# Gate, up and down projections as seven products of half size in place of eight, in a hybrid decoder layer on one core

## The chip, the core and the metric

The kernel runs on one core of a Trainium2 chip. The core has TensorE (PE; PEld is its weight load), VectorE (DVE), ScalarE (ACT), GpSimd (POOL), SyncE (SP, which only issues transfers here) and 16 DMA engines. [...] The metric is device time in microseconds (us); the median of a few runs counts.

## The reference

One decoder layer in float32: 512 tokens, width 2048, inner width 5632. The first half (two mixing branches and their output projection) is not changed. The second half is

```
h = modulate(rms_norm(x, norm_ffn_g[l]), sh_f, sc_f)
gate, up = jnp.split(h @ w_gu[l], 2, axis=-1)
x = x + g_f[:, None, :] * ((jax.nn.silu(gate) * up) @ w_down[l])
...
return rms_norm(x, final_norm_g)
```

`modulate` is h * (1 + scale) + shift. Shift, scale and the gate g_f are columns of silu(c) @ w_ada + b_ada, one value for each feature.

## The kernel before

Features lie on partitions, the 512 tokens (S) on the free axis; the width is 16 tiles of 128 (KT), the inner width 44 (FT). Each float32 operand is split into two float32r parts, hi and lo, and a product is three matmuls, hi by hi, hi by lo, lo by hi (`mm3`, L124 to L126). SP loads a weight block (`wraw`, L115), ACT casts it to `whi` (L105), DVE subtracts it to `wlo` (L106).

`channel` does the second half. It first puts half of the output projection on x1 (`project`, weights `w_out`; DVE adds the gated result to x1, `square` sums squares). Beside it, `mod_steps` works out columns 68 to 79 of the modulation: a load `adaq` and a DVE product with accumulation (L199) for each quarter column. Then `norm` gives 1/rms in PSUM, and `modulate` makes hi and lo of h (L247, L251, L252). Four chunks of the inner width follow: for eleven tiles each, gate and up (16 k-tiles, weights stationary, 512 tokens moving), Silu on ACT, product and split; then 16 output tiles of the down projection over the chunk's eleven k-tiles, added to x1 with the gate (L969). PSUM accumulators take turns over three tags. After the last chunk come `norm` again, the final scaling (L975) and a write of each x1 tile (L977).

Pools: `big` is 32 tiles of 128 x 512 (x1, the mixing half's operands, later h). The weights have pool `wm` (512 columns, three buffers), and from the norm on pool `wf` (1024 columns; two raw buffers, three of hi and of lo). Instructions stand on each engine in the order that a scheduler gives them, from program order, priorities (the splits of weights have high priority) and buffers that come free; each engine then works its queue in order.

## Time and profile before

| | us |
|---|---|
| median of 3 runs | 2512.97 |
| lowest, highest run | 2510.55, 2514.32 |
| span of the profiled execution | 2515.8 |
| start of the gate/up part (first matmul) | 1046.0 |
| last large matmul | 2494.2 |

The span is what one profiled execution took from its first to its last instruction; it lies 2.8 us above the median. A row of a group reads: line, engine, operation, output<-inputs with shapes and count, then busy time and mean ns of one, then idle time before it and what ended it. A row of the timeline reads: start, duration, engine, line, operation, and in brackets the idle time before and its releaser. The page gives a granted TensorE clock of 0.986 of full speed over the span; most of what is missing lies in the mixing half and at the end.

### The profile page before, as it was taken

What the parts mean: (1) busy time and instruction counts of PE and PEld (TensorE: products, weight loads), DVE (VectorE), ACT (ScalarE), POOL (GpSimd) and SP (SyncE); (2) the same over time, 40 slices, a digit from 0 to 9 for tenths busy, and PEclk for the clock granted to TensorE, in tenths of its full rate; (3) what the DMA queues carried; (4) which work ended last, traced back from release to release, by engine and by line L of the source; (5) the groups of instructions that cost most, each with busy time, mean ns of one, the idle gap of its engine ahead of it and who ended that gap; (6) DMA issues with size and microseconds to landing.
All of it is one profiled execution on the core that took longest, in us unless ns stands there. A gap on an engine that the chain in (4) does not pass through costs nothing.

```text
span 2515.8 us, 30983 instructions
## 1 busy us (share of the span) xinstructions
PE 2413.9 (96%) x11560; PEld 1953.4 (78%) x11560; DVE 1380.4 (55%) x3111; ACT 843.7 (34%) x1340; POOL 82.0 (3%) x131
## 2 busy tenths in 40 slices
PE   5999999999999999899999999999999999999997
PEld 3677777877777886687788888888888888888885
DVE  7979898999969847854423322233322233222244
ACT  4357364455355333432222222222222222222221
POOL 0000111111101000000000000000000000000000
PEclk9999998999999999999999999999999999999998
DMA  8864444444342438366423332323333233333233
GB/s 304 308 219 130 148 128 143 131 152 144 125 135 81 143 108 283 119 195 194 160 90 95 108 100 93 101 83 98 106 98 99 89 92 105 101 93 100 85 95 112
DMA packets 138938, 333.22 MB, mean 132 GB/s; under 512 B 15458, under 2 KB 28898, under 8 KB 134690
## 3 DMA queue, kind: packets, MB, share of 16 engines
q1 hardware_dynamic: 138788, 331.25, 40.7%
q8 instruction: 90, 1.47, 0.2%
q14 instruction: 60, 0.49, 0.1%
HBM read 322.92 MB, written 7.87 MB: 131 GB/s over the span
## 4 chain that ended last, share of the span: by engine, by line
PE 72%; DVE 9%; DMA 7%; issue 1%; ACT 1%; SPq 0%; POOL 0%; DVEq 0%; ACTq 0%
PE ps_mm L124 10%; PE ps_mm L126 10%; PE ps_mm L125 10%; PE ps_gr L126 6%; PE ps_st L124 6%; PE ps_gr L124 6%; PE ps_st L126 6%; PE ps_gr L125 6%; PE ps_st L125 6%; DMA adaq<-in_w_ada 6%; DVE adaq L199 2%; DVE wlo L106 2%; DVE rw_xp L764 1%; DVE rw_x L766 1%; DMA wraw<-in_w_out 1%
## 5 line engine op out<-in xcount | busy, mean ns | idle before, releaser
L106 DVE TENSOR_TENSOR wlo<-wraw,whi 128x1024 fp32r<-128x1024 f32 (+2 forms) x552 | 496.7, 902 | 730.2 <-ACT whi L105 721.1
L105 ACT CAST whi<-wraw 128x1024 fp32r<-128x1024 f32 (+2 forms) x552 | 436.6, 792 | 1292.4 <-PE ps_mm L125 401.1
L124 PE MATMUL ps_mm<-hhi,whi 128*128 128x512 f32 x1020 | 417.1, 410 | 9.8 <-ACT hhi L251 7.2
L126 PE MATMUL ps_mm<-hhi,wlo 128*128 128x512 f32 x1020 | 407.2, 399 | 1.7 <-DVE wlo L106 1.6
L125 PE MATMUL ps_mm<-hlo,whi 128*128 128x512 f32 x1020 | 406.5, 399 | 0.8 <-DVE hlo L252 0.7
L124 PEld LDWEIGHTS ps_mm<-hhi,whi 128*128 128x128 f32 x1020 | 193.4, 190 | 53.2 <-ACT hhi L251 9.9
L125 PEld LDWEIGHTS ps_mm<-hlo,whi 128*128 128x128 f32 x1020 | 193.7, 190 | 43.4 <-DVE hlo L252 4.8
L126 PEld LDWEIGHTS ps_mm<-hhi,wlo 128*128 128x128 f32 x1020 | 193.8, 190 | 42.3 <-DVE wlo L106 3.0
L199 DVE SCALAR_TENSOR_TENSOR adaq<-adaq,cbq 128x512 f32<-128x512 f32 x256 | 173.5, 687 | 92.9 <-DMA adaq<-in_w_ada 85.1
L126 PE MATMUL ps_gr<-hhi,wlo 128*128 128x512 f32 x496 | 193.7, 390 | 3.1 <-DVE wlo L106 3.1
L126 PE MATMUL ps_st<-hhi,wlo 128*128 128x512 f32 x496 | 193.6, 390 | 2.0 <-DVE wlo L106 2.0
L124 PE MATMUL ps_st<-hhi,whi 128*128 128x512 f32 x496 | 194.0, 391 | 1.6 <-ACT hhi L251 1.6
L125 PE MATMUL ps_gr<-hlo,whi 128*128 128x512 f32 x496 | 193.5, 390 | 0.0
L125 PE MATMUL ps_st<-hlo,whi 128*128 128x512 f32 x496 | 193.5, 390 | 0.0
L124 PE MATMUL ps_gr<-hhi,whi 128*128 128x512 f32 x496 | 192.6, 391 | 0.0
L126 PEld LDWEIGHTS ps_gr<-hhi,wlo 128*128 128x128 f32 x496 | 93.4, 188 | 23.6 <-DVE wlo L106 4.1
L126 PEld LDWEIGHTS ps_st<-hhi,wlo 128*128 128x128 f32 x496 | 93.4, 188 | 21.8 <-DVE wlo L106 2.5
L124 PEld LDWEIGHTS ps_st<-hhi,whi 128*128 128x128 f32 x496 | 93.5, 188 | 21.6 <-ACT hhi L251 2.2
L125 PEld LDWEIGHTS ps_gr<-hlo,whi 128*128 128x128 f32 x496 | 93.7, 189 | 19.6
L124 PEld LDWEIGHTS ps_gr<-hhi,whi 128*128 128x128 f32 x496 | 93.7, 189 | 19.4
L125 PEld LDWEIGHTS ps_st<-hlo,whi 128*128 128x128 f32 x496 | 93.3, 188 | 19.8 <-DVE hlo L252 0.3
L766 DVE TENSOR_TENSOR rw_x<-rw_x,rw_xp 128x27 f32<-128x27 f32 (+23 forms) x496 | 94.7, 196 | 5.7
(312 smaller groups left out, 3809.6 us busy)
## 6 DMA issues: line engine op xcount, KB each, us to landing
wraw<-in_w_gu SPq DMA_DIRECT2D x176, 512.0 KB, 3.6
adaq<-in_w_ada SPq DMA_DIRECT2D x256, 256.0 KB, 3.3
wraw<-in_w_in SPq DMA_DIRECT2D x160, 256.0 KB, 3.0
ada<-in_w_ada SPq DMA_DIRECT2D x32, 1024.0 KB, 7.2
wraw<-in_w_down SPq DMA_DIRECT2D x64, 512.0 KB, 3.5
wraw<-in_w_out SPq DMA_DIRECT2D x64, 256.0 KB, 3.3
wraw<-in_w_down SPq DMA_DIRECT2D x64, 192.0 KB, 2.3
x<-in_x SPq DMA_DIRECT2D x32, 256.0 KB, 5.3
```

The lines of the kernel that those rows point to most:

```text
L105: nc.scalar.copy(out=hi, in_=src)
L106: nc.vector.tensor_tensor(out=lo, in0=src, in1=hi.bitcast(F32), op=ALU.subtract)
L124: mm(ps, lhsT=w[0], rhs=x[0], start=start, stop=False)
L125: mm(ps, lhsT=w[0], rhs=x[1], start=False, stop=False)
L126: self.pe = mm(ps, lhsT=w[1], rhs=x[0], start=False, stop=stop).ins
L199: nc.vector.scalar_tensor_tensor(out=t, in0=t, scalar=1.0, in1=cb, op0=ALU.mult, op1=ALU.mult, accum_out=part[:, m, h:h + 1])
L764: tt(out=pr[:, :n, :j], in0=at[:, s + 1:, s:s + 1].to_broadcast([P, n, j]), in1=x[:, s:s + 1, :j].to_broadcast([P, n, j]), op=ALU.mult)
L766: tt(out=x[:, s + 1:, :j], in0=x[:, s + 1:, :j], in1=pr[:, :n, :j], op=ALU.add)
```

## The change

Gate/up and down are now done by a Strassen-Winograd form. A and B are cut into two by two blocks: A by tokens (256 each) and by k, B by k and by columns. Seven products of half size replace eight; their operands are sums of blocks, and the results are sums of products.

The operands change places: 128 k x 128 tokens of an activation operand are stationary, 128 k x 512 columns of weights move, so results come with tokens on partitions. A "block" m is 512 columns of gate and the same 512 of up (eleven blocks, eight k-tiles for each half of K), or for down two blocks of 2 x 512 output columns in each of three chunks of K (8, 7 and 7 k-tiles per half). `half` does a block in two passes of steps of two k-tiles: products 1, 6, 5, 4, then 7, 2, 3. Each step loads weights (512 KB a load, four in the first pass, three in the second), adds them on DVE (`wraw<-wraw,wraw`, L1269, L1270, L1276 and L1285), splits each product's operand and issues twelve matmuls (L1227 to L1229), six for each of two token tiles. `finish` takes products out of PSUM: p1 by ACT (L1237), the others by DVE (p6 L1240, p5 L1243, p4 L1246, p7 L1249 and L1250, p2 L1254, p3 L1257). Products 1 and 7 share two PSUM banks, 6 and 2 two, 5 and 3 two, 4 has two.

The activation operands are built once: for h in the first block, with subtractions on POOL (`h_first`, `h_second`), for the silu products (which go to DRAM and come back, `from_s`) during the last block of the stage before. As results now lie by tokens, the silu products and x1 are transposed on PE (`flip`: four transposes, an ACT copy, a write to DRAM): sixteen groups for x1 beside the output projection, four for each gate/up block in the next block's first step. Down results of the three chunks are added through DRAM (`yd`, POOL, L1091); with the last chunk come the gate as a row of DRAM (`gf`, L1096), x1 read back (L1097), and the squares (ACT); after all, the scalings (L1172) and writes. Columns 80 to 95 of the modulation are worked out during gate/up. The pool `wm` is closed before the second half of the output projection, and `wf` has eight raw buffers and four of hi and lo. The weights are packed in the new blocks, and the output is by tokens. The rest of the diff takes comments out and puts `big` into eight tiles of four.

```diff
@@ channel @@
+        self.wmctx.close()
+        self.open_weights(ctx, "wf", 1024, 8, 4)
...
-        self.open_weights(ctx, "wf", 1024, 2, 3)
...
+        def flip(dst, tag, srcs):
+            ps = self.ps(tag)
+            for z, v in enumerate(srcs):
+                nc.tensor.transpose(ps[:, z * P:(z + 1) * P], in_=v, identity=self.con("ident"))
+            t = fq.tile([P, S], F32, tag="ft", name="flip", bufs=2)
+            nc.scalar.copy(out=t, in_=ps)
+            nc.sync.dma_start(out=dst, in_=t)
+        def flip_x1(e):
+            for t in range(4):
+                flip(self.x1d[t][e], "ch", [xt[4 * e + z][:, t * P:(t + 1) * P] for z in range(4)])
...
+            def done(m):
+                self.square(acc, xt[m], m, fp)
+                if m % 4 == 3 and m < KT - 1:
+                    flip_x1(m // 4)
...
-                pg, pu = ps(), ps()
-                self.gemm(pg, i["w_gu"][2 * m], h)
-                self.gemm(pu, i["w_gu"][2 * m + 1], h)
-                t = fp.tile([P, S], F32, tag="ft", name="sil", bufs=2)
-                act(out=t, in_=pg, func=AF.Silu)
-                p = ps()
-                self.gemm(p, i["w_down"][cf, m], s)
-                stt(out=xt[m], in0=p, scalar=self.mod[:, 80 + m:81 + m], in1=xt[m],
-                    op0=ALU.mult, op1=ALU.add)
...
+            rstd = self.norm(acc, "ch")
+            flip_x1(3)
...
+        def h_first(j):
+            q, z = j // 2, slice(2 * (j % 2), 2 * (j % 2) + 2)
+            for a in (q, 2 + q):
+                for k in range(z.start, z.stop):
+                    v, kk = quads[a][:, k], 4 * a + k
+                    stt(out=v, in0=v, scalar=self.cols[:, 16 + kk:17 + kk], in1=rstd, op0=ALU.mult, op1=ALU.mult)
+                    nc.scalar.activation(out=v, in_=v, func=AF.Identity, bias=self.mod[:, 48 + kk:49 + kk])
+            a11, a21 = quads[q][:, z, :256], quads[q][:, z, 256:]
+            a22 = quads[2 + q][:, z, 256:]
+            t = self.staging()
+            s1, s2 = t[:, :2], t[:, 2:]
+            pool_tt(out=s1, in0=a21, in1=a22, op=ALU.subtract)
+            pool_tt(out=s2, in0=s1, in1=a11, op=ALU.subtract)
+            ops = stages[0]["ops"]
+            for p, v in ((1, a11), (4, a22), (5, s1), (6, s2)):
+                if j % 2 == 0:
+                    ops[p, q] = self.operand_tile(p)
+                self.split_into(ops[p, q][:, 0, z], ops[p, q][:, 1, z], v)
...
+        def from_s(st, c, q, second):
...
+                a11 = load(0, 0)
+                operand(1, a11)
+                a21, a22 = load(0, 1), load(1, 1)
+                operand(4, a22)
+                pool_tt(out=a21, in0=a21, in1=a22, op=ALU.subtract)
+                pool_tt(out=a11, in0=a21, in1=a11, op=ALU.subtract)
+                operand(5, a21)
...
+        def gu_end(m, a, v, w, u, t):
+            act = nc.scalar.activation
+            if u is not None:
+                act(out=w, in_=w, func=AF.Silu)
+                tt(out=w, in0=w, in1=u, op=ALU.mult)
+                self.sT[t + 2] = w
...
+                    rows = list(self.sT)
+                    def pending(z):
+                        flip(where[4 * m + z], ("st", "y")[z % 2], [r[:, z * P:(z + 1) * P] for r in rows])
...
+        def fetch(src, tag):
+            t = fq.tile([P, S], F32, tag=tag[0], name="fetch", bufs=tag[1])
+            nc.sync.dma_start(out=t, in_=src)
+            return t
+        def down_end(c):
+            def put(x, t, e):
+                if c:
+                    pool_tt(out=x, in0=x, in1=fetch(yd[t][e], ("ft", 2)), op=ALU.add)
+                if c < 2:
+                    nc.sync.dma_start(out=yd[t][e], in_=x)
+                    return
+                g = fetch(self.gf[:, e * S:(e + 1) * S].to_broadcast([P, S]), ("ad", 2))
+                tt(out=x, in0=x, in1=g, op=ALU.mult)
+                tt(out=x, in0=x, in1=fetch(self.x1d[t][e], ("ft", 2)), op=ALU.add)
+                junk = fq.tile([P, S], F32, tag="ad", name="junk", bufs=2)
+                nc.scalar.activation(out=junk, in_=x, func=AF.Square, accum_out=ss[:, t, e:e + 1])
+                if e % 2 == 0:
+                    nc.sync.dma_start(out=self.xd[t][e // 2], in_=x)
+                else:
+                    kept[t, e] = x
...
+        stages = [dict(n=8, count=11, src=gu_src, end=gu_end, ops={})]
+        for c in range(3):
+            stages.append(dict(n=chunks[c][1], count=2, src=down_src(c), end=down_end(c), ops={}))
...
+        for z, st in enumerate(stages):
+            for m in range(st["count"]):
+                final = m == st["count"] - 1
+                for second in (False, True):
+                    if not z and not m and second:
+                        h_second()
+                    steps = self.half(st, m, second)
+                    for j in range(4):
+                        if not z and not m and not second:
+                            h_first(j)
+                        next(steps)
+                        if final and z + 1 < len(stages) and j % 2:
+                            from_s(stages[z + 1], z, j // 2, second)
+                        if z == 0 and m:
+                            next(mods, 0)
...
+        r = self.small.tile([P, 4], F32, tag="rstd", name="rstd", bufs=1)
+        nc.vector.tensor_reduce(out=r, in_=ss, op=ALU.add, axis=AX.X)
+        nc.scalar.activation(out=r, in_=r, func=AF.Sqrt, scale=1.0 / D, bias=self.eps[:, 0:1])
+        nc.vector.reciprocal(out=r, in_=r)
+        for t in (2, 3, 0, 1):
+            for e in range(4):
+                x = kept[t, e]
+                stt(out=x, in0=x, scalar=r[:, t:t + 1], in1=fg[:, e], op0=ALU.mult, op1=ALU.mult)
+                nc.sync.dma_start(out=self.out[t, :, e * S:(e + 1) * S], in_=x)
@@ new functions of Layer @@
+    def half(self, stage, m, second):
...
+        tags = {1: ("mm", "mm"), 6: ("gr", "gr"), 5: ("ch", "ch"), 4: ("st", "y"),
+                7: ("mm", "mm"), 2: ("gr", "gr"), 3: ("ch", "ch")}
...
+        def product(p, b, k0, w):
+            with tc.high_priority():
+                hi = self.wp.tile([P, self.wc], F32R, tag="whi", name="whi", bufs=self.wb[1])
+                lo = self.wp.tile([P, self.wc], F32R, tag="wlo", name="wlo", bufs=self.wb[1])
+                hi, lo = (t.rearrange("p (k n) -> p k n", n=S)[:, :w] for t in (hi, lo))
+                self.split_into(hi, lo, b)
+            o = stage["ops"][p, k0 // 4]
+            if k0 == 0:
+                ps[p] = [self.ps(tags[p][t]) for t in range(2)]
+            for t in range(2):
+                for z in range(w):
+                    k = k0 + z
+                    ah, al = (o[:, h, k % 4, t * P:(t + 1) * P] for h in range(2))
+                    mm(ps[p][t], lhsT=ah, rhs=hi[:, z], start=k == 0, stop=False)
+                    mm(ps[p][t], lhsT=al, rhs=hi[:, z], start=False, stop=False)
+                    mm(ps[p][t], lhsT=ah, rhs=lo[:, z], start=False, stop=k == n - 1)
+                if k0 + w == n:
+                    finish(p, t)
+        def finish(p, t):
+            keep, q = self.keep, ps[p][t]
+            if p == 1:
+                x = keep["a", t] = tmp("a", t)
+                nc.scalar.copy(out=x, in_=q)
+            elif p == 6:
+                x = keep["b", t] = tmp("b", t)
+                tt(out=x, in0=q, in1=keep["a", t], op=ALU.add)
+            elif p == 5:
+                x = keep["v", t] = tmp("v", t)
+                tt(out=x, in0=q, in1=keep["b", t], op=ALU.subtract)
+            elif p == 4:
+                x = keep["w", t] = tmp("w", t)
+                tt(out=x, in0=q, in1=keep["b", t], op=ALU.add)
+            elif p == 7:
+                u, v, w = tmp("b", t), keep["v", t], keep["w", t]
+                tt(out=w, in0=q, in1=w, op=ALU.add)
+                tt(out=u, in0=v, in1=q, op=ALU.subtract)
+                stage["end"](m, None, None, w, u, t)
+            elif p == 2:
+                x = keep["a", t]
+                tt(out=x, in0=q, in1=x, op=ALU.add)
+            else:
+                x = keep["v", t]
+                tt(out=x, in0=q, in1=x, op=ALU.add)
+                stage["end"](m, keep["a", t], x, None, None, t)
+        for k0 in range(0, n, 2):
+            w = min(2, n - k0)
+            flips = None
+            if not second and k0 == 0:
+                flips, self.pending = self.pending, None
+            if not second:
+                b11, b12, b22, b21 = (load(z, k0, w) for z in (0, 2, 3, 1))
+                product(1, b11, k0, w)
+                with tc.high_priority():
+                    tt(out=b11, in0=b11, in1=b12, op=ALU.add)
+                    tt(out=b12, in0=b11, in1=b22, op=ALU.add)
+                product(6, b12, k0, w)
+                if flips:
+                    flips(0)
+                    flips(1)
+                with tc.high_priority():
+                    tt(out=b21, in0=b21, in1=b12, op=ALU.add)
+                product(5, b11, k0, w)
+                if flips:
+                    flips(2)
+                    flips(3)
+                product(4, b21, k0, w)
+            else:
+                b12, b22, b21 = (load(z, k0, w) for z in (2, 3, 1))
+                with tc.high_priority():
+                    tt(out=b12, in0=b12, in1=b22, op=ALU.add)
+                product(7, b12, k0, w)
+                product(2, b21, k0, w)
+                product(3, b22, k0, w)
+            yield```

On DVE, at the change from one gate/up block to the next (`wraw_11133`, `_11135`, `_11137`, `_11139` are the new block's first weights; `ps_mm_10900` and `_10901` are product 7 of the block before, `wlo_11112` is the lo part of its product 3), the changed kernel has:

```order
L106 TENSOR_TENSOR wlo_11112<-wraw_11062,whi_11111 128x1024
L106 TENSOR_TENSOR wlo_11142<-wraw_11133,whi_11141 128x1024
L1249 TENSOR_TENSOR ev_w_10851<-ps_mm_10900,ev_w_10851 128x512
L1269 TENSOR_TENSOR wraw_11133<-wraw_11133,wraw_11135 128x1024
L1250 TENSOR_TENSOR ev_b_11077<-ev_v_10831,ps_mm_10900 128x512
L1270 TENSOR_TENSOR wraw_11135<-wraw_11133,wraw_11137 128x1024
L1064 TENSOR_TENSOR ev_w_10851<-ev_w_10851,ev_b_11077 128x512
L1276 TENSOR_TENSOR wraw_11139<-wraw_11139,wraw_11135 128x1024
L106 TENSOR_TENSOR wlo_11162<-wraw_11135,whi_11161 128x1024
L106 TENSOR_TENSOR wlo_11197<-wraw_11133,whi_11196 128x1024
L106 TENSOR_TENSOR wlo_11231<-wraw_11139,whi_11230 128x1024
L1249 TENSOR_TENSOR ev_w_10859<-ps_mm_10901,ev_w_10859 128x512
```

The second tile of product 7 leaves PSUM (last row) behind four splits and three additions of the new block's weights. On PE, at the same place, the new block's first products stand directly behind product 3:

```order
L1229 MATMUL ps_ch_10937<-wlo_11112,comb_10886 128x512
L1227 MATMUL ps_mm_11145<-whi_11141,comb_10464 128x512
...
L1229 MATMUL ps_mm_11145<-wlo_11142,comb_10464 128x512
L1227 MATMUL ps_mm_11146<-whi_11141,comb_10464 128x512
L1228 MATMUL ps_mm_11146<-whi_11141,comb_10464 128x512
```

`ps_mm_11146` takes the bank of `ps_mm_10901`. Before, DVE had at the end of a gate/up pair one product (L958) between splits, and the next accumulator was another bank:

```order
L106 TENSOR_TENSOR wlo_11831<-wraw_11828,whi_11830 128x1024
L958 TENSOR_TENSOR sil_11789<-sil_11789,ps_gr_11668 128x512
L106 TENSOR_TENSOR wlo_11861<-wraw_11858,whi_11860 128x1024
L106 TENSOR_TENSOR slo_11793<-sil_11789,shi_11792 128x512
L106 TENSOR_TENSOR wlo_11891<-wraw_11888,whi_11890 128x1024
```

On SP, at the end of the output projection and the start of gate/up, before:

```order
L115 DMA wraw_9752<-in_w_out 128x512
L115 DMA wraw_10508<-in_w_gu 128x1024
...
L115 DMA wraw_10252<-in_w_out 128x512
L115 DMA wraw_10538<-in_w_gu 128x1024
L115 DMA wraw_10270<-in_w_out 128x512
L115 DMA wraw_10568<-in_w_gu 128x1024
```

and in the changed kernel (`x1d03` to `x1d33` are the writes of the last flips of x1):

```order
L943 DMA x1d03_9430<-flip_10381 128x512
L198 DMA adaq_12579<-in_w_ada 128x512
L943 DMA x1d13_9434<-flip_10389 128x512
L1211 DMA wraw_10476<-in_w_gu 128x2x512
L943 DMA x1d23_9438<-flip_10397 128x512
L943 DMA x1d33_9442<-flip_10405 128x512
L1211 DMA wraw_10478<-in_w_gu 128x2x512
L1211 DMA wraw_10480<-in_w_gu 128x2x512
L1211 DMA wraw_10482<-in_w_gu 128x2x512
```

The first gate/up weights stood among the loads of `w_out`; now they stand behind the last writes of x1.

More of the change, by code (lines that the diff above doesn't have):

```diff
@@ L973, in channel @@
-        rstd = self.norm(acc, "ch")
-        for k in range(KT):
-            stt(out=xt[k], in0=xt[k], scalar=self.vec("final_norm_g", k), in1=rstd,
-                op0=ALU.mult, op1=ALU.mult)
-            nc.sync.dma_start(out=self.out[:, k], in_=xt[k])
+        def flip(dst, tag, srcs):
[5 more added lines that the diff above has]
+            nc.sync.dma_start(out=dst, in_=t)
```

223 lines of the change are left out of this document (161 added, 62 removed).

## The prediction

> **What bounds the kernel now.** First the page's head and its chain of work that ended last; then the windows, engine by engine.
>
> ```profile
> span 2515.8 us, 30983 instructions
> PE 2413.9 (96%) x11560; PEld 1953.4 (78%) x11560; DVE 1380.4 (55%) x3111; ACT 843.7 (34%) x1340; POOL 82.0 (3%) x131
> ...
> PE 72%; DVE 9%; DMA 7%; issue 1%; ACT 1%; SPq 0%; POOL 0%; DVEq 0%; ACTq 0%
> ```
>
> TensorE (PE) is busy nearly always. A share over the whole span hides stages, so two windows (span start and width, then busy time and count of PE, PEld, DVE, ACT, POOL, then clock, DMA share, GB/s):
>
> ```profile
> 400.00:600.00 200.00, 192.15 (x1129) 152.29 (x1129) 183.11 (x610) 103.66 (x199) 21.45 (x31) 0.97 0.47 147
> 1400.00:1600.00 200.00, 200.00 (x884) 165.61 (x883) 58.96 (x58) 48.09 (x55) 0.00 (x0) 1.00 0.31 99
> ```
>
> In the gate/up/down part PE has no gap: 200 us over 884 matmuls is 0.2262 us each, VectorE (DVE) is busy 29%, POOL not at all. Fewer matmuls are worth their full time there, as long as another engine does not become the bound. The other window shows how dense DVE gets in this kernel: 92%, never 100%.
>
> **The change, part by part.** *Matmuls.* Gate, up and down issue (1408 + 704) x 3 = 6336 matmuls of 512 columns; seven products for eight leave 5544, of the same 512 columns. 792 x 0.2262 = **179 us** less. All else is cost.
>
> *DVE.* Its rows:
>
> ```profile
> L106 DVE TENSOR_TENSOR wlo<-wraw,whi 128x1024 fp32r<-128x1024 f32 x239 | 292.6, 1225 | 451.8 <-ACT whi L105 445.8
> L105 ACT CAST whi<-wraw 128x1024 fp32r<-128x1024 f32 x239 | 251.7, 1054 | 786.2 <-PE ps_gr L125 196.7 <-PE ps_st L125 196.1 <-PE ps_mm L125 191.8
> L958 DVE TENSOR_TENSOR sil<-sil,ps_st 128x512 f32<-128x512 f32 x15 | 10.3, 687 | 42.7 <-PE ps_st L126 42.7
> ```
> ```profile
> 1059.18 2.36 DVE L106 TENSOR_TENSOR wlo<-wraw,whi 128x1024 fp32r<-128x1024 f32 x2 [1.83 <-ACT whi L105]
> ...
> 2501.37 10.62 DVE L975 SCALAR_TENSOR_TENSOR x<-x,vecs,ps_ch 128x512 f32<-128x512 f32 x16 [1.58 <-PE ps_ch L240]
> ```
>
> Two subtractions in a row end 2.36 - 1.225 = 1.135 us apart, sixteen operations of 512 take 10.62, 0.664 each: these are the rates in a full queue. A column block m of gate/up (eight k-tiles) has four steps, each with seven splits and four additions of weights, 44 x 1.135 = 49.9 us, and 18 operations of 512 (evictions L1237 to L1257, silu products), 11.9: **DVE needs 61.8**. PE needs 28 products x 12 matmuls = 336 x 0.2262 = **76.0**. Blocks m1 to m9 stay with PE (six adaq operations beside them do not change that). For a down block of seven k-tiles it is 294 x 0.2262 = 66.5 against 54.
>
> *Transposes.* Sixteen groups of four for x1, 44 for the silu products:
>
> ```profile
> 219.35 0.48 PE L124 MATMUL ps_mm<-lru_uhi,whi 128*128 128x512 f32 x1
> 219.67 0.62 PE L655 MATMUL ps_st<-cons,bd_b 128*128 128x128 f32 x4
> 220.05 0.48 PE L125 MATMUL ps_mm<-lru_ulo,whi 128*128 128x512 f32 x1
> ```
>
> Four 128x128 products between two large ones spread these from 0.226 to 0.70 us: 0.47 a group, 1.9 a block.
>
> *The wait at a block's end (L1249, L1250).* Products 1 and 7 share the PSUM tag "mm". The next block's product 1, second token tile, cannot start until DVE has taken product 7's second tile out. In DVE's order L1249 and L1250 of that tile stand behind the split of the new block's product 4, and that split needs a free hi/lo buffer, that is the end of product 3. So: product 3 ends, ACT casts (1.054), DVE subtracts (1.225, or 1.135), L1249 and L1250 (0.66 each): about 3.7. PE has six matmuls of the first tile to do meanwhile, 1.36; it stands about **2.5 us** per block (0 if the queue lets the evictions through sooner, 3.7 with no cover). A block of eight: 76.0 + 1.9 + 2.5 = 80.4; of seven: 69.0.
>
> *The stage's start.* Now:
>
> ```profile
> 955.69 0.43 SPq L115 DMA_DIRECT2D wraw<-in_w_gu  x1
> ...
> 1013.62 0.42 SPq L115 DMA_DIRECT2D wraw<-in_w_gu  x1
> ...
> 1044.48 1.41 DVE L247 SCALAR_TENSOR_TENSOR modt<-x,cols,ps_ch 128x512 f32<-128x512 f32 x2 [1.06 <-PE ps_ch L240]
> ...
> 1046.04 0.80 PE L124 MATMUL ps_st<-hhi,whi 128*128 128x512 f32 x1 [1.59 <-ACT hhi L251]
> ```
> ```profile
> 1000.00:1010.00 10.00, 9.27 (x40) 7.04 (x39) 7.84 (x18) 3.61 (x6) 0.00 (x0) 1.00 0.92 311
> ...
> wraw<-in_w_gu SPq DMA_DIRECT2D x176, 512.0 KB, 3.6
> yraw<-y SPq DMA_DIRECT2D x14, 256.0 KB, 2.8
> ```
>
> The norm is ready at 1044.5, and the first weights were loaded 30 to 90 us before. In the changed order SP issues the first weight block behind the write of x1d13 and the next three behind x1d33, and these writes wait for transposes that PE does after the norm. Twelve other x1 writes (256 KB each, 3.1 MB, 10 us at 311 GB/s) go into a stretch where the transfers are 92% busy: I put the norm 5 us later, at **1049.5** (0 to 10). From there four flips, copy and issue, about 4, and 3.6 of landing put the first product at +9; products 6 to 4 follow +11 late. DVE then has 61.8, 32 operations of 512 to build h's operands (21.1) and 6 of 1024 (6.8), 89.7 in all, of which some 4 lie in that wait: m0 takes 8 + 89.7 - 4 = **94**, bound by DVE.
>
> *POOL.* It now adds and subtracts two SBUF tensors: 10.2k elements a partition in m0, 10.2k in m10 and 9k in the first down chunk's second block (building the next operands), 13k in the second chunk's, 4.1k in each block of the third. No row has such an operation. The nearest:
>
> ```profile
> L616 POOL TENSOR_SCALAR bd_a<-rw_ar 64x256 f32<-64x256 f32 x32 | 34.6, 1081 | 256.9 <-DVE rw_xp L764 122.7 <-DVE rw_ar L609 106.9 <-PE ps_mm L124 13.7
> L775 POOL TENSOR_SCALAR bd_xt<-rw_xs 32x128 f32<-32x128 f32 x64 | 39.9, 623 | 287.2 <-DVE rw_xs L771 142.1 <-DVE rw_xp L764 123.9 <-DVE rw_x L766 17.8
> ```
> ```profile
> 560.58 1.77 POOL L616 TENSOR_SCALAR bd_a<-rw_ar 64x256 f32<-64x256 f32 x2 [0.22 <-PE ps_st L587]
> ```
> ```profile
> 213.39 2.97 POOL L616 TENSOR_SCALAR bd_a<-rw_ar 64x256 f32<-64x256 f32 x2 [23.34 <-DVE rw_ar L609]
> ...
> 213.83 0.69 DVE L590 TENSOR_TENSOR rw_a<-rw_a,rw_kk 128x512 f32<-128x512 f32 x1
> ...
> 214.43 0.89 DVE L584 SCALAR_TENSOR_TENSOR rw_t<-mix_r,vecs,mix_k 128x512 f32<-128x512 f32 x1
> ```
>
> A pair took 1.77 us, but 2.97 beside DVE; and a DVE operation beside it 0.89, the one before 0.69. So both stand: DVE 0.20 per POOL operation of 256 elements with one input, 0.8 ns an element; with two inputs up to 1.6. The two POOL sizes (0.623 at 128 elements, 0.885 at 256) give 2.05 ns an element and 0.36 fixed, 2.46 us for 1024. If DVE stood for all of it, 2.4 ns an element. Let h be that standstill: 0 to 2.4; I take **1.2**, midway between the row's two readings. It counts where DVE is the bound or close to it: m10 has 61.8 + 14 operand splits (15.9) = 77.7, the first chunk's last block 74, the second's 69, each block of the third 64.5.
>
> [...]
>
> *The end.* Before:
>
> ```profile
> 2494.22 0.39 PE L126 MATMUL ps_gr<-shi,wlo 128*128 128x512 f32 x1
> ...
> 2494.65 0.75 DVE L969 SCALAR_TENSOR_TENSOR x<-ps_gr,mod,x 128x512 f32<-128x512 f32 x1 [5.28 <-PE ps_gr L126]
> ...
> 2496.14 1.28 ACT L233 ACT_TABLE_LOAD   x1
> ```
>
> From the last matmul's start to the span's end is 21.6. After: eight results of the last half, each with a fetch of yd (2.8) into two "ft" buffers, a POOL add (1.4 by the line above), a product with gf and an addition of x1d, which fetches into the same two buffers. That is a chain of 8 x 4.2 = 33.6, of which 3.4 lie beside products 2 and 3; then 2.0 for the last product, addition and square, 1.8 for table load and rstd, and from the first of sixteen scalings to the end 14.4 as before (2515.8 - 2501.4). **48.4**, 27 more (10 if the fetches run ahead, 35 if nothing lies beside the products).
>
> **The sum**, against the span of 2515.8, which stands 2.8 above the median of the runs shown (2512.97): norm 1049.5; m0 94 + 12.2 (10.2k x 1.2); m1 to m9 9 x 80.4 = 723.6; m10 77.7 + 12.2 = 89.9; first chunk 80.4 and 74.2 + 10.8 = 85.0; second 69.0 and 69 + 15.6 = 84.6; third 2 x (64.5 + 4.9) = 138.8; end 48.4: 2475.4. A queue was never over 92 to 96% full; 4% of the 366 us bound by DVE adds 14.6: 2490. Less 2.8: **2487 us**. The same sum, with PE's time where that is longer, at h = 0: 2434; 0.8: 2469; 1.6: 2508; 2.4: 2553.
>
> **Rivals.** *POOL holds DVE (slower).* If DVE stands for the whole of each POOL operation, h = 2.4 gives 2553; the point where it turns is h = 1.69, 2513. For it: both engines lengthen where they meet. Against it: 0.20 of 0.885 us. *POOL costs DVE almost nothing:* h at or under 0.3 and PE everywhere the bound: 2434 to 2447; with the waits at the blocks' ends gone too (16 x 2.5) 2394. For it: the engine that lengthened most in the row is POOL (1.2 us of a pair, DVE 0.2), and POOL has slack. *Nothing moves:* h between 1.6 and 1.78 (2508 to 2518). *Transfers set the late blocks:* the second chunk's last moves 23 MB (12.8 of weights, 6.4 of operands, 4.2 of yd), 74 us at 311 GB/s, which the sum's 84.6 covers; at half that rate it would add 63, and 2550 is reached. That the matmuls do not go is excluded by the rows of the order.
>
> **How the numbers follow.** Forecast (h 0.4 to 1.6, 2450 to 2508): 0.53. POOL nearly free: 0.19. No change (within 0.2%, 5 us, about what a measurement can tell from none): 0.07. Slower by POOL holding DVE: 0.17; by transfers or an unseen wait: 0.04. Faster 0.72, same 0.07, slower 0.21. The range leaves out one in ten below and one above: 2425 to 2550.
>
> **What would show it.** Right: 0.226 us a matmul in m1 to m9, and a PE gap of about 2.5 us with L1250 as its releaser once a block; the first weights of the stage behind the x1d writes; DVE above 90% in m0 and m10 and wlo groups lengthened there only while POOL runs; 40 to 50 us behind the last matmul. Wrong: PE gaps in m1 to m9 that wait for wraw or for wlo all through a block; a DVE that stands for whole POOL operations (wlo of 3 us); a norm later than 1060.

## The result, and the profile after

The changed kernel takes **2638.81 us** (median of 4 runs, 2630.03 to 2646.73); the kernel before, on the same chip, 2511.84 (4 runs, 2510.55 to 2514.32). The ratio is 1.051 (95% interval 1.048 to 1.053): **slower by 127 us**, where 26 us faster was forecast. The time lies outside the range (2425 to 2550) as well.

The head of the page, and four windows: from the norm to the end of m0, m1 to m5 (adaq loads beside them), m6 to m9, and m10 with the six down blocks. Here and below a block ends where DVE starts the last L1250 of its product 7. Columns as in the prediction's windows.

```profile
span 2634.3 us, 32326 instructions
PE 2345.7 (89%) x10992; PEld 1856.6 (70%) x10992; DVE 2096.4 (80%) x3730; ACT 1117.4 (42%) x1625; POOL 260.1 (10%) x207
```
```profile
1072.53:1196.40 123.87, 93.62 (x358) 72.58 (x356) 103.07 (x104) 62.56 (x78) 35.54 (x14) 0.84 0.55 178
1196.40:1628.40 432.00, 409.19 (x1760) 330.66 (x1760) 340.70 (x405) 172.59 (x190) 0.00 (x0) 0.97 0.66 211
1628.40:1957.00 328.60, 318.60 (x1408) 257.60 (x1408) 250.93 (x249) 137.93 (x152) 0.00 (x0) 1.00 0.60 192
1957.00:2574.50 617.50, 547.58 (x2210) 426.95 (x2210) 501.71 (x467) 241.73 (x279) 132.52 (x55) 0.94 0.68 223
```

The same stage of the kernel before, in one window:

```profile
1046.00:2494.00 1448.00, 1440.22 (x6335) 1189.55 (x6336) 499.22 (x626) 347.33 (x420) 0.00 (x0) 1.00 0.34 106
```

The stage lost its 792 matmuls and still went from 1448 to 1502 us. Before, PE stood for 8 us of it, at a clock of 1.00 but for 4 us at the stage's start. Now it stands for 133 (1502 less the four busy times), and the clock falls in three of the four windows. DVE is not full either: 83%, 79%, 76% and 81%. Neither engine is the bound; they wait for each other. PE's waits in the stage (total us, times, longest) say for whom:

```profile
PE ps_gr L1227 <- ACT whi L105: 35.3, 11, 14.1
PE ps_mm L1227 <- DVE ev_b L1250: 34.4, 13, 5.8
PE ps_mm L1227 <- ACT whi L105: 13.1, 5, 4.0
PE ps_gr L1229 <- DVE wlo L106: 9.8, 9, 2.5
PE ps_mm L1229 <- DVE wlo L106: 9.5, 7, 4.2
```

The 1502 us split as follows. 5544 matmuls at 0.2267 (the spacing measured alone, below) are 1257. They stand 0.2307 apart here, which is 22 more. The 44 flips are 18 (0.40 each, by the starts of the matmuls around them). PE stands 133. What is left is 72, most of it matmuls at half clock: one minus the clock, times the width, sums over the four windows to 20 + 13 + 0 + 37 = 70, but part of that is idle time. PE was busy in 107 us of the stretches at half clock, so they cost 54; the last 18 have no cause shown. The rows after a long wait show the half clock:

```profile
2420.05 0.80 PE L1227 MATMUL ps_gr<-whi,comb 128*128 128x512 f32 x1 [8.62 <-ACT whi L105]
2420.65 0.63 PE L1228 MATMUL ps_gr<-whi,comb 128*128 128x512 f32 x1
2421.08 0.63 PE L1227 MATMUL ps_gr<-whi,comb 128*128 128x512 f32 x1
...
2423.38 0.39 PE L1229 MATMUL ps_gr<-wlo,comb 128*128 128x512 f32 x1
2423.61 0.39 PE L1227 MATMUL ps_gr<-whi,comb 128*128 128x512 f32 x1
```

Starts are 0.43 us apart for 3 us, then 0.23.

Against the prediction's sum for the profiled execution (2490): norm 1072.5 (+23); m0 123.9 for 106.2, or 110.4 with its 4% (+13.5); m1 to m9 760.6 for 723.6 (+37); m10 88.1 for 93.5 (-5); first chunk +7; second +11.5; third and end +57 (45 of it the third chunk, 183.4 for 138.8). Together 144.

### The profile page after: what moved, and what is told of

The parts are those of the page before. It is cut to its first block, busy times and chain, and to the rows that moved or that the text cites. A ratio compares the mean times of both kernels' runs of the same rounds, so it can differ in the third digit from the quotient of the medians.

```text
span 2634.3 us, 32326 instructions
## 1 busy us (share of the span) xinstructions
PE 2345.7 (89%) x10992; PEld 1856.6 (70%) x10992; DVE 2096.4 (80%) x3730; ACT 1117.4 (42%) x1625; POOL 260.1 (10%) x207
## 5 line engine op out<-in xcount | busy, mean ns | idle before, releaser
L105 ACT CAST whi<-wraw 128x1024 fp32r<-128x1024 f32 (+1 forms) x707 | 625.9, 901 | 908.2 <-DVE wraw L1270 250.8
L106 DVE TENSOR_TENSOR wlo<-wraw,whi 128x1024 fp32r<-128x1024 f32 (+1 forms) x707 | 742.0, 1067 | 245.3 <-ACT whi L105 240.9
L1227 PE MATMUL ps_mm<-whi,comb 128*128 128x512 f32 x528 | 216.7, 411 | 53.7 <-DVE ev_b L1250 34.4
L1227 PE MATMUL ps_gr<-whi,comb 128*128 128x512 f32 x528 | 217.7, 412 | 36.1 <-ACT whi L105 35.3
L124 PE MATMUL ps_mm<-hhi,whi 128*128 128x512 f32 x556 | 235.7, 426 | 8.4 <-ACT hhi L255 6.7
L199 DVE SCALAR_TENSOR_TENSOR adaq<-adaq,cbq 128x512 f32<-128x512 f32 x256 | 174.4, 688 | 73.4 <-DMA adaq<-in_w_ada 59.5
L126 PE MATMUL ps_mm<-hhi,wlo 128*128 128x512 f32 x556 | 225.9, 406 | 0.0
L1229 PE MATMUL ps_gr<-wlo,comb 128*128 128x512 f32 x528 | 214.4, 408 | 9.8 <-DVE wlo L106 9.8
L1229 PE MATMUL ps_mm<-wlo,comb 128*128 128x512 f32 x528 | 214.6, 407 | 9.5 <-DVE wlo L106 9.5
L1227 PE MATMUL ps_ch<-whi,comb 128*128 128x512 f32 x528 | 210.7, 399 | 5.1 <-DVE x L996 2.5
L1228 PE MATMUL ps_gr<-whi,comb 128*128 128x512 f32 x528 | 214.3, 406 | 0.0
L1228 PE MATMUL ps_mm<-whi,comb 128*128 128x512 f32 x528 | 214.2, 406 | 0.0
L1229 PE MATMUL ps_ch<-wlo,comb 128*128 128x512 f32 x528 | 209.4, 397 | 1.9 <-DVE wlo L106 1.9
L1228 PE MATMUL ps_ch<-whi,comb 128*128 128x512 f32 x528 | 209.9, 398 | 0.0
L1227 PEld LDWEIGHTS ps_mm<-whi,comb 128*128 128x128 f32 x528 | 103.6, 196 | 83.4 <-DVE ev_b L1250 38.4
L1227 PEld LDWEIGHTS ps_gr<-whi,comb 128*128 128x128 f32 x528 | 104.2, 197 | 65.1 <-ACT whi L105 40.3
L1229 PEld LDWEIGHTS ps_gr<-wlo,comb 128*128 128x128 f32 x528 | 103.3, 196 | 39.4 <-DVE wlo L106 15.5
L1229 PEld LDWEIGHTS ps_mm<-wlo,comb 128*128 128x128 f32 x528 | 103.5, 196 | 35.1 <-DVE wlo L106 12.9
L1227 PEld LDWEIGHTS ps_ch<-whi,comb 128*128 128x128 f32 x528 | 101.0, 191 | 31.1 <-DVE ev_v L1257 4.2
```

The lines of the kernel that those rows point to most:

```text
L105: nc.scalar.copy(out=hi, in_=src)
L106: nc.vector.tensor_tensor(out=lo, in0=src, in1=hi.bitcast(F32), op=ALU.subtract)
L124: mm(ps, lhsT=w[0], rhs=x[0], start=start, stop=False)
L126: self.pe = mm(ps, lhsT=w[1], rhs=x[0], start=False, stop=stop).ins
L199: nc.vector.scalar_tensor_tensor(out=t, in0=t, scalar=1.0, in1=cb, op0=ALU.mult, op1=ALU.mult, accum_out=part[:, m, h:h + 1])
L1227: mm(ps[p][t], lhsT=ah, rhs=hi[:, z], start=k == 0, stop=False)
```

## The experiments

The theory at this point: the DVE work that was counted as hidden is not hidden. In each step a chain runs in order (load, additions on DVE, cast on ACT, subtraction on DVE, matmuls) through four hi/lo buffers, with evictions, operand splits and adaq products queued between its links, and each stop of PE costs some half clock on top. The rivals: the wait at L1250 alone; the flips; the transfers; POOL alone. Each run below is compared with the kernel before on the same chip, and with the 2638.8 of the changed kernel, whose own four runs lie 17 us apart.

**e1, product 7's evictions ahead in DVE's queue.**

```diff
-                tt(out=w, in0=q, in1=w, op=ALU.add)
-                tt(out=u, in0=v, in1=q, op=ALU.subtract)
+                with tc.high_priority():
+                    tt(out=w, in0=q, in1=w, op=ALU.add)
+                    tt(out=u, in0=v, in1=q, op=ALU.subtract)
```

> Product 7's two subtractions get high priority, so that DVE does them ahead of the next block's splits. Theory (the wait at each block's end is one of DVE's order, 2.4 us in quiet blocks, 6.8 beside the adaq loads, and a slower clock after the long ones): blocks m1 to m5 fall from 85-88 us to about 80, m6 to m9 from 82 to 79.6, the PE idle time that L1250 ends (34 us) goes to under 5, the whole is 35 to 50 us shorter than 2638, about 2595. Rival (DVE's queue is simply full, the wait comes back as a wait for wlo or whi): PE's idle time moves to other releasers, less than 10 us gained.

2633.3 us, ratio 1.048 (1.046 to 1.050). The waits for L1250 are gone. That gave some 5 us, not 34, and even these are not clear of noise: the four runs (2630.6 to 2634.2) lie inside the spread of the changed kernel's. Two places from PE's timeline, first of the changed kernel, then of e1:

```profile
1285.38 0.80 PE L1227 MATMUL ps_mm<-whi,comb 128*128 128x512 f32 x1 [5.75 <-DVE ev_b L1250]
...
1711.11 0.50 PE L1227 MATMUL ps_mm<-whi,comb 128*128 128x512 f32 x1 [2.36 <-DVE ev_b L1250]
```
```profile
1705.15 0.50 PE L1227 MATMUL ps_mm<-whi,comb 128*128 128x512 f32 x1 [0.95 <-ACT whi L105]
```

In a quiet block the wait was 2.36 us, as the prediction worked out (2.5). In blocks with adaq loads it was up to 5.75 (not the 6.8 of the expectation). With it gone the next link is late: a quiet block falls only from 82.0 to 81.6 us, since PE then waits for the cast. Over the stage, the waits of `ps_mm` for the cast rise from 13.1 to 26.4 us. The wait that ends last is not the only one that is late.

**e2 and e6, the x1 flips.** e2 issues them one output tile later; e6 also gives them eight copy buffers of their own and two PSUM tags.

```diff
-                if m % 4 == 3 and m < KT - 1:
-                    flip_x1(m // 4)
+                if m % 4 == 0 and m:
+                    flip_x1(m // 4 - 1)
```

> The first three groups of x1 transposes are put one tile later in the output projection. Theory (in each group PE waits 2.5 us for the addition of the tile it has just finished, then runs 3.4 us at half clock): the three waits of 2.4 to 2.6 us go, the norm is ready at about 1060 instead of 1072, the whole is 10 to 14 us shorter. Rival (the projection is paced by the adaq and weight transfers on one queue): the waits move to whi or wraw, the norm stays within 4 us of 1072.

> x1 transposes one tile later as in the run before, and with eight buffers of their own and two PSUM tags. Theory (a group of four waits for its ACT copies, and these for the writes to DRAM of the two shared buffers): the waits of 3 to 5 us in each group go; from the first product of the output projection's second half to the norm it takes under 112 us where it took 125, the whole is 10 to 18 us shorter than 2638. Rival (weight and adaq loads pace this stretch): over 120 us there, under 5 us gained.

2637.7 (1.047 to 1.053) and 2639.4 (1.046 to 1.053): nothing. **e11** leaves out the x1 flips and their writes before the norm (the last chunk reads the input x in place of x1).

> Leaves out the sixteen groups of x1 transposes and their writes; the last additions read the input x from DRAM in their place (same sizes). Theory (the writes and the queue order at the start of gate/up cost what the norm came late by): the norm at about 1060, the first gate/up product 4 us behind it where it was 10, 15 to 25 us shorter. Rival (weight and adaq loads pace the stretch whatever the flips do): the norm within 5 us of the 1072 to 1083 of the other runs, 5 to 10 us shorter.

2623.8 us (1.043 to 1.049), 15 less. The last large matmul of the projection ended 10 us sooner, but the norm came only 3 us sooner; PE stood:

```profile
1064.37 1.87 PE L230 MATMUL ps_ch<-ones,sqacc 128*128 128x1 f32 x8 [13.35 <-DVE sqacc L223]
```

DVE's timeline of the changed kernel shows what the last sum of squares (L223) stands behind:

```profile
1061.94 0.69 DVE L199 SCALAR_TENSOR_TENSOR adaq<-adaq,cbq 128x512 f32<-128x512 f32 x1 [0.52 <-DMA adaq<-in_w_ada]
...
1063.70 0.69 DVE L199 SCALAR_TENSOR_TENSOR adaq<-adaq,cbq 128x512 f32<-128x512 f32 x1 [1.06 <-DMA adaq<-in_w_ada]
1064.32 0.08 DVE L199 DVE_READ_ACCUMULATOR adaq<-adaq,cbq 128x1 f32 x1
1064.32 0.75 DVE L462 SCALAR_TENSOR_TENSOR x<-ps_mm,mod,x 128x512 f32<-128x512 f32 x1
...
1066.18 0.69 DVE L223 TENSOR_TENSOR sqacc<-sqacc,sqt 128x512 f32<-128x512 f32 x1
```

These adaq products belong to columns 80 to 95. The scheduler has drawn them ahead of the norm, in DVE's order, and each waits for a load into one of two buffers, one per 1.9 us. From the start of the projection's last matmul to the norm it takes 6.3 us before, 11.8 in the changed kernel, 19.3 in e11, and 6.8 in e5 (next), which has none of these products.

**e5, columns 80 to 95 left out** (gate of the down results set to zero).

```diff
-        mods = self.mod_steps(range(80, 96), fq, ("cb", 1, "ad", 2))
+        mods = iter(())
+        nc.vector.memset(self.mod[:, 80:96], 0.0)
```

> Leaves out columns 80 to 95 of the modulation (their 64 loads and products beside gate/up; the gate row is zero). Theory (these loads and the 0.69 us DVE operations fall into blocks m1 to m5 and make their boundary waits 6.8 us instead of 2.4, with slower clock after): m1 to m5 fall from 85-88 us to the 82 of m6 to m9, the first weights come some us earlier, 20 to 30 us shorter in all. Rival (those blocks are long by their own weight loads or splits): under 8 us.

2622.0 us (1.042 to 1.048), 17 less; m1 to m5 fell from 432.0 together to 414.0. The norm did not come sooner (1079.8).

**e3, the squares' scratch output in the buffer "cb".**

```diff
-                junk = fq.tile([P, S], F32, tag="ad", name="junk", bufs=2)
+                junk = fq.tile([P, S], F32, tag="cb", name="junk", bufs=1)
```

> The scratch output of the last squares leaves the two buffers in which the gf row is fetched. Theory (each of the last sixteen results is a chain of 6.1 us because the next gf fetch waits for the square before it): the spacing at the end falls to about 4, the end behind the last large matmul from 61 to about 45 us, and the pass before it gains 5 to 15: 20 to 30 us shorter in all. Rival (the yd and x1d fetches into two other buffers set the spacing): under 6 us.

2614.6 us (1.037 to 1.044), 24 less for one buffer. DVE's products with gf at the end, in the changed kernel:

```profile
2591.99 0.69 DVE L1096 TENSOR_TENSOR ev_b<-ev_b,fetch 128x512 f32<-128x512 f32 x1 [5.44 <-DMA fetch<-gf]
...
2598.15 0.69 DVE L1096 TENSOR_TENSOR ev_a<-ev_a,fetch 128x512 f32<-128x512 f32 x1 [3.65 <-DMA fetch<-gf]
...
2604.00 0.69 DVE L1096 TENSOR_TENSOR ev_v<-ev_v,fetch 128x512 f32<-128x512 f32 x1 [3.33 <-DMA fetch<-gf]
```

and in e3:

```profile
2576.91 0.69 DVE L1096 TENSOR_TENSOR ev_b<-ev_b,fetch 128x512 f32<-128x512 f32 x1 [2.46 <-POOL ev_b L1091]
...
2580.94 0.69 DVE L1096 TENSOR_TENSOR ev_a<-ev_a,fetch 128x512 f32<-128x512 f32 x1 [2.50 <-POOL ev_a L1091]
...
2585.03 0.69 DVE L1096 TENSOR_TENSOR ev_v<-ev_v,fetch 128x512 f32<-128x512 f32 x1 [2.39 <-POOL ev_v L1091]
```

The links were 6 us apart, since the fetch of gf shared two buffers with the scratch output and so waited for the Square of the result before. They are now 4.1 apart, the prediction's 4.2. From the last matmul to the end it is 46.0 us (60.7 before this edit; forecast 48.4).

**e8, e3 with the down results' fetches and writes issued by POOL** (the fetch is shown; the two writes are changed alike).

```diff
-            nc.sync.dma_start(out=t, in_=src)
+            nc.gpsimd.dma_start(out=t, in_=src)
```

> As the run with the scratch output moved, and the fetches and writes of the down results are issued by POOL in place of SP. Theory (weight loads stand in SP's queue behind a write that waits for POOL's addition, so the third chunk's blocks start late): its first block falls from 95 to about 80, the second chunk's second from 90 to about 82, together 15 to 25 us beyond that run's 2614. Rival (DVE's queue, where a product waits for its gf row ahead of the splits): within 6 us of 2614.

2622.1 us (1.041 to 1.049): not better than e3. The third chunk's first block, where a gain was expected, stays at 94.3 us (95.7 in e3), and its second rises from 75.3 to 89.7. Nothing here points to SP's queue; but on POOL the issues stand behind POOL's own additions, so the run does not exclude it.

**e4, no POOL subtractions for the down operands** (the five lines of `from_s` left out: operands 5 to 7 and 3 are not the sums that they should be).

```diff
-                pool_tt(out=a21, in0=a21, in1=a22, op=ALU.subtract)
-                pool_tt(out=a11, in0=a21, in1=a11, op=ALU.subtract)
...
```

> Leaves out the subtractions on POOL that build the down operands from the silu products (28 thousand elements a partition; the down result is not the reference's); the operands are split and used as before. Theory (DVE stands still about 1.4 ns for each of their elements, and the operand splits wait for POOL): m10, the first chunk's second block and the second chunk's second block are 8 to 15 us shorter each, 25 to 40 in all. [...]

2595.1 us (1.031 to 1.036), 44 less for 28.2 thousand elements a partition: 1.6 ns each, where h was put at 1.2 (0 to 2.4). The operand splits no longer wait for POOL either, and the 1.6 includes that. Blocks fell where the subtractions had been: m10 from 88.1 to 80.7, the second chunk's last from 90.7 to 80.8. POOL's timeline of the changed kernel in m0, at a place where DVE is idle (1139.9 to 1148.9), gives the price of one alone:

```profile
1142.11 2.34 POOL L1018 TENSOR_TENSOR stage<-x 128x1024 f32<-128x1024 f32 x1
```

What one beside DVE does is in two timelines of the changed kernel, DVE's:

```profile
2068.06 1.22 DVE L106 TENSOR_TENSOR wlo<-wraw,whi 128x1024 fp32r<-128x1024 f32 x1
2069.31 3.29 DVE L1269 TENSOR_TENSOR wraw<-wraw 128x1024 f32<-128x1024 f32 x1
```

and POOL's:

```profile
2067.14 4.38 POOL L1054 TENSOR_TENSOR stage<-stage 128x1024 f32<-128x1024 f32 x1 [25.44 <-DVE comb L106]
2071.60 3.27 POOL L1055 TENSOR_TENSOR stage<-stage 128x1024 f32<-128x1024 f32 x1
```

POOL's first operation takes 4.38 where L1018 took 2.34: it stands until DVE's subtraction ends at 2069.28. Then it has its turn, and DVE's addition stands until POOL ends at 2071.52 and takes its own 1.1 after that: 3.29 in place of 1.22. In these rows the exclusion is whole, in both directions, where the prediction read a part (0.20 of 0.885 us) from a row with one-input operations. Beside a DVE that read PSUM, neither engine lengthened here: an addition of 512 on POOL (L1091, at 2575.55) took 1.27 us (the shortest of its 32 is 1.26, the longest 2.36) while DVE did L1254 twice in 1.28 (0.68 each at the median).

**e7, the weight additions left out** (L1269, L1270, L1276, L1285; the products get unsummed blocks).

```diff
-                    tt(out=b11, in0=b11, in1=b12, op=ALU.add)
-                    tt(out=b12, in0=b11, in1=b22, op=ALU.add)
...
-                    tt(out=b21, in0=b21, in1=b12, op=ALU.add)
...
-                    tt(out=b12, in0=b12, in1=b22, op=ALU.add)
```

> Leaves out the four additions of weights in each step (1.2 us of DVE each; products are of unsummed weights). Theory (DVE's work and its order in the queue make the waits): m6 to m9 fall from 82 to under 80, m0, m10 and the blocks of the chunks lose 5 to 15 us each, 70 to 110 us in all, about 2545. If the spacing of matmuls falls from 0.2307 back to 0.2267, DVE's traffic set it; if not, it is something else. Rival (transfers on SP's queue make the waits): under 30 us.

2542.8 us, ratio 1.012 (1.009 to 1.015): **96 less**, the largest single part. A quiet block falls from 82.0 to 79.5 us. Most of the gain is where DVE had more to do: m0 falls from 123.9 to 105.5, m1 to m9 by 33 (24 of it in m1 to m5), the first chunk by 11, the second by 10, the third by 29. The waits for L1250 fall from 34.4 to 3.0 us:

```profile
PE ps_mm L1227 <- ACT whi L105: 10.2, 4, 3.7
PE ps_mm L1229 <- DVE wlo L106: 9.6, 5, 7.0
...
PE ps_mm L1227 <- DVE ev_b L1250: 3.0, 5, 0.9
```

The additions of 1024 columns are 331 us of DVE's time in the changed kernel's groups (four lines; the first and the last of them here):

```profile
L1269 DVE TENSOR_TENSOR wraw<-wraw 128x1024 f32<-128x1024 f32 x64 | 84.7, 1324 | 0.5
...
L1285 DVE TENSOR_TENSOR wraw<-wraw 128x1024 f32<-128x1024 f32 x64 | 79.6, 1243 | 29.0 <-DMA wraw<-in_w_gu 18.8 <-DMA wraw<-in_w_down 9.3 <-DVE wlo L106 0.5
```

DVE was full in none of the four windows, yet leaving them out is worth 96 us. The run takes away their time and also the link between load and cast, and does not tell the two apart.

**e10, everything at once:** e1, e3, e4, e5 and e7 together.

> Leaves out the weight additions, the POOL subtractions of the down operands and columns 80 to 95 of the modulation, and has the two edits for product 7 and for the scratch output: what is left is the 5544 matmuls, splits, evictions, transposes and transfers. Theory (the side work of the seven products is what eats their saving): gate/up blocks of 79.5, down blocks of 68 to 80, the whole about 2450, so 60 us faster than before. Rival (transfers or PE's own order hold it as well): above 2490.

2480.8 us, ratio 0.988 (0.986 to 0.991). **e12** is e1 with e3, and computes all of the layer.

> The two edits that keep the result, product 7's high priority and the scratch output in a buffer of its own, together. If their gains add: 2638 - 24 - 5 = about 2609; if the earlier eviction frees DVE for the results at the end, 2600; if they overlap, 2614. All stay above 2512.

2609.3 us (1.037 to 1.043), 5 under e3, but the runs of the two overlap (2606.9 to 2616.4 and 2608.5 to 2616.9), so whether the gains add up is not shown. Of the versions that leave nothing out none has a lower time, and all are slower than the kernel before.

**e9, e13 and e14: the matmuls' spacing.** It is 0.2307 us on average in the changed kernel and 0.2267 before. e9 is the kernel *before* with every weight block of the second half loaded twice:

```diff
+        if self.extra is not None:
+            t = self.extra.tile([P, 1024], F32, tag="ex", name="extra", bufs=1)
+            self.nc.sync.dma_start(out=t[:, :n], in_=src)
```

> The kernel before, with every weight block of gate/up and down loaded a second time into a buffer that nothing reads (99 GB/s become about 200, as in the changed kernel). Theory (the denser transfers slow each matmul, 0.2267 to 0.2307 us): the spacing rises to 0.229-0.231 and the time by 15 to 30 us, to about 2535. Rival (it is not the transfers; weights as the moving side, or ACT and DVE writing what PE reads): the spacing stays 0.2267, the time within 5 us of 2512.

2577.9 us (1.024 to 1.031), but the spacing stays 0.2270 at 218 GB/s; the window shows PE standing for 4 of 200 us, since the weights come late on the one queue (in it ACT waited 159 us for loads of `wraw`; in the kernel before no wait for a load is listed there):

```profile
1400.00:1600.00 200.00, 195.91 (x848) 157.76 (x848) 54.99 (x56) 45.11 (x52) 0.00 (x0) 1.00 0.65 218
```

e13 and e14 issue matmuls alone, five series of 288 each; e14 also runs casts on ACT and subtractions on DVE beside some of them:

```diff
+        def casts(n):
+            for z in range(n):
+                nc.scalar.copy(out=sw[z % 2], in_=flat[z % 4])
+        def subs(n):
+            for z in range(n):
+                nc.vector.tensor_tensor(out=sv[z % 2], in0=flat[z % 4], in1=flat[(z + 1) % 4], op=ALU.subtract)
```

> Only matmuls (the layer is left out, the output is no result of it): five series of 288 with 512 columns, nothing else running. First the operand layout of before, 48 matmuls to a PSUM bank; second the layout of the changed kernel (activation tiles stationary as hi, lo, hi, weights moving as hi, hi, lo), 6 to a bank; third before's layout, 6 to a bank; fourth the changed layout, 48 to a bank; fifth the changed layout in the order hi, hi, lo, 48 to a bank. If the order or layout of the operands sets 0.2307 us, series two, four and perhaps five show it and one and three show 0.2267; if the change of banks does, two and three; if all show 0.2267, it is the company of the other engines in the kernel.

> Matmuls alone again (outputs are not the reference's: nothing of the layer is computed), five series of 288 in the changed kernel's layout, one after the other; beside them: series 1 nothing; series 2 ACT casts of 128x1024 into a buffer of their own; series 3 DVE subtractions of 128x1024 from two buffers into a third; series 4 both; series 5 nothing. What this measures is the wider spacing of the matmuls in the changed kernel (0.2307 us against 0.2267, some 20 us of the whole), which neither the layout, nor the transfers, nor the weight additions explained. Theory, that PE shares SBUF with an ACT and a DVE that write operands beside it: series 2, 3 or 4 is spaced 0.230 or more, 1 and 5 0.2267. Rival, that the spacing does not come from other engines' work: all five at 0.2267.

361.3 and 364.7 us (one run each). In both every stretch is spaced 0.2266 to 0.2267. Windows of e14 with both engines busy, and with neither:

```profile
30.00:65.00 35.00, 35.00 (x156) 28.98 (x155) 34.04 (x29) 33.98 (x33) 0.00 (x0) 1.00 0.00 1
...
120.00:150.00 30.00, 30.00 (x134) 24.84 (x133) 0.00 (x0) 0.00 (x0) 0.00 (x0) 1.00 0.00 1
```

(The scheduler drew part of the side work forward into the first series; it covers stretches with both, with either and with none.) So neither the layout, nor the turn of the PSUM banks, nor ACT and DVE beside PE makes it by itself, nor transfers in the kernel before; e7 excludes the additions (0.2302 without them).

The changed kernel's trace says where to look. The 0.2307 is a mean of two spacings that go by the product. Twelve matmuls of product 6 and the twelve of product 5 behind them, in m6:

```profile
1654.75:1657.47 2.72, 2.72 (x14) 2.25 (x12) 1.62 (x2) 1.05 (x1) 0.00 (x0) 1.00 0.92 331
1657.47:1660.27 2.80, 2.80 (x14) 2.26 (x12) 2.77 (x3) 0.00 (x0) 0.00 (x0) 1.00 0.42 157
```

Products 6 and 7 stand 0.2266 apart, products 2, 4 and 5 stand 0.2332, in gate/up and down, here and in e1 to e8 and e10 to e12 alike. Products 1 and 3 begin at the wider spacing only where they follow one of these three, and end at 0.2266. Just 2, 4 and 5 have their stationary operands in the pool `cp` (L1189), the others in `big` (L1191). PSUM banks do not divide them so (6 and 2 share theirs), nor do the weights' buffers, which take turns. What it is about `cp` stays open: no run moves an operand from one pool to the other, and e13 and e14 had theirs in one pool.

## Why the prediction was wrong

**The step that failed: "Blocks m1 to m9 stay with PE (six adaq operations beside them do not change that)", with DVE's 61.8 us against PE's 76.0, and the same for the down blocks, 54 against 66.5.** The comparison of two engines' needs was taken for the time, and the additions were thereby costed at nothing outside the blocks that were counted as bound by DVE. They cost 96 us (e7): 18 in m0, which was counted as bound by DVE, but also 33 in m1 to m9 and 29 in the third chunk. The adaq products cost 17 (e5). In the quiet blocks the step held: m6 to m9 took 328.6 for 321.6, and some 5 of the 7 are the spacing. In m1 to m5 it was 432.0 for 402.0, and e5 gives back 18 of these 30. DVE at three quarters of its time still decides when PE can go on. The account that fits the rows is that its work stands in order on a chain that PE needs at fixed points, with few buffers to let one run ahead of the other; no run changes the number of buffers, so that part is argued. The prediction asked what covers each edit, and named PE's 76.0 as the cover; a cover holds only if the hidden engine can run ahead by as much as its densest stretch, and that stretch was not looked for. It is at a block's end, in DVE's timeline of the changed kernel (end of m1):

```profile
1279.51 1.22 DVE L1276 TENSOR_TENSOR wraw<-wraw 128x1024 f32<-128x1024 f32 x1
1280.64 3.49 DVE L106 TENSOR_TENSOR wlo<-wraw,whi 128x1024 fp32r<-128x1024 f32 x3
1284.05 0.68 DVE L1249 TENSOR_TENSOR ev_w<-ps_mm,ev_w 128x512 f32<-128x512 f32 x1
1284.65 0.68 DVE L1250 TENSOR_TENSOR ev_b<-ev_v,ps_mm 128x512 f32<-128x512 f32 x1
```

PE stops at 1279.63, and ahead of L1250 three splits are still to be done, not the one of the prediction: PE's wait is 5.75 us and not 2.36, and the clock is at 0.50 from 1283.01 to 1289.84. Without the adaq products the longest such wait in these blocks is 2.4 (e5).

**The half clock was not in the sum at all.** The prediction's stalls were priced at their own length. It cost 54 us of the stage by the clock's records; the kernel before, with 8 us of stalls, lost 2, at the stage's start.

**Matmuls removed: right** in number (the count on PE's line falls from 11560 to 10992, transposes included), wrong in price by the spacing: 22 us. It goes with the pool that holds the stationary operand; the cause is open.

**The wait at a block's end: right** in mechanism and size in a quiet block (2.36 for 2.5; its own terms, 3.6 less 1.36, come to 2.2), and worth little by itself (e1).

**The flips: near**, 0.40 each for 0.47. **The norm: mis-sized.** 1072.5 where 1049.5 (0 to 10 added) was put. Most of it lies ahead of the norm: the projection's last large matmul started at 1060.7, and before at 1038.2. Without the x1 flips the projection ended 10 us sooner (e11), and the adaq products drawn ahead then held the norm back. But with the same code up to there the norm lay between 1072.5 and 1083.2 in the profiles (e1, e3, e4, e7), and without those adaq products at 1079.8 (e5) and 1086.7 (e10), so what makes up the 23 us is not settled.

**m0: mis-sized**, 123.9 for 110.4. PE's longest wait, 14.1 us for a cast, lies there.

**POOL against DVE: mis-sized, at the edge of the forecast's own range, and for the wrong reason.** h = 1.2 was chosen and about 1.6 measured (e4, with the splits' wait for POOL in it), worth 21 us by the prediction's own sum. But in the rows shown under e4 the exclusion is whole (3.29 us for 1.22), not a fraction. That h comes out below 2.4 fits that some of POOL's operations meet a DVE that is idle or reads PSUM, and that in others POOL is the one that waits; how many of each was not counted. The row that the 0.20 came from was also misread: L584 takes 0.75 at its median, not the 0.69 of another operation, so DVE stood 0.13 there. The rival "POOL holds DVE", with h above 1.69 as its turning point, is not what made the kernel slower: with the POOL work of the down operands gone it still takes 2595.

**The third chunk** is the largest single miss: 183.4 for 138.8. The additions are 29 of the 45 (e7), the shared scratch buffer 13 (e3).

**The end: mechanism right, one term mis-sized.** The chain of eight was put at 4.2 a link; 6.1 was measured, because the prediction counted the two "ft" buffers and overlooked that gf's two are shared with the scratch output. With that undone it is 4.1 (e3).

**The rivals.** None of them was what happened. "Transfers or an unseen wait" had 0.04 and should have had far more: the unseen wait was the common case. The 4% allowance for queues that are never full was laid on 366 us only, those that counted as bound by DVE; on the stage's whole 1378 it would have been 55, of 144 missing.

**Could it have paid?** e10 takes away all of the side work that could be taken away, and gains 31 us of the 179 against before. The other 148: flips 18 and spacing 19 (5544 at 0.2302); the norm 42 later (1086.7 for 1044.5); an end of 45.7 for 21.6, 24; m0 some 22 above a quiet block; the rest, some 23, not divided further. So even with this side work gone the change gives back 88 of its 179 at the norm, in m0 and at the end.

## What to carry to other kernels

Compare needs per engine to find a candidate for the bound, but price added work on a second engine by the chain that it lies in: which links stand in one in-order queue, how many buffers lie between, and what else is queued there when the step ends. Here the kernel whose bound engine had hardly a gap (8 of 1448 us) had hardly a clock loss (2 us); in the changed kernel, beside their own length, some of the stalls of 2 us or more had 3.41 us or a multiple at a clock of 0.50 behind them. Before arithmetic is traded for side work, list everything that goes through each shared buffer tag; one scratch output cost 24 us here.
